# Split weights and stationary tiles that begin at staggered byte offsets in a float32r transformer chain

## The chip, the cores and the metric

The kernel runs on one core of a Trainium2 chip. The metric is the device time of one execution in microseconds (us), median over the runs. TensorE multiplies, ScalarE and VectorE do elementwise work, GpSimd does a few small operations, and SyncE issues most of the transfers. SBUF is the on-chip memory, 128 partitions side by side; an address here is a byte offset within a partition, the same in all of them.

## The reference, cut to what matters

The computation is three transformer layers in a row on 256 tokens of width 1024: a layer with window and neighbourhood attention and an MLP, a layer with retention and an MLP, and a hybrid layer with three attention branches. For the change only their dense products matter, which all have this form:

```python
h = _rmsnorm(x, norm_g)
z = h @ w_in
x = x + y @ w_out
x = x + jnp.square(jax.nn.relu(h @ w1)) @ w2
```

All data are float32. The weights amount to some 42 million numbers and each is used once per execution, for 256 tokens.

## The kernel before, in words

**Split products.** A float32 product is computed as three products in the format float32r, which keeps fewer bits: a number a is split in a_hi (rounded) and a_lo (the rest), and a times b is taken as a_hi b_hi + a_hi b_lo + a_lo b_hi. `mm3` (L329) issues the three matmuls in this order: xh with wh, xh with wl, xl with wh. The activations are the stationary operand (a tile of 128 x 128, loaded by a weight-load instruction ahead of its matmul), and the weights stream past it (128 rows, mostly 512 columns). So in every matmul of a dense layer a slice of `xh` or `xl` (or `hh`, `hl` in the second product of an MLP) is loaded and a slice of a `whi` or `wlo` buffer is streamed.

**Weights.** `plan` (L347) lists the weights in order of use in pieces of 4 x 512 columns (a few of 4 x 256 and 4 x 328). `w_dma` (L392) loads a piece to one of four `raw` buffers over SyncE's queue. A piece is split in two halves, each with two k-tiles. `w_hi` (L424) rounds a half with ScalarE to one of five `whi` buffers, `w_lo` (L438) subtracts with VectorE to one of five `wlo` buffers. `w_get` (L459) hands the slices to the products: the first k-tile of a half begins at column 0 of the buffer, the second at column w (512, 256 or 328). `w_done` (L470) frees a half when the last of the 256 tokens has used it.

**Products.** `panel` (L477) computes 512 output columns (256 or 328 in places) for both token tiles t = 0, 1: k-tiles in groups of two, two and four, for t = 0 and then t = 1. `proj` (L509) and `mlp_out` (L1082) do the products whose k-tiles come in groups of four, with four accumulators. `h_task` (L1051) makes the inner activations of an MLP: ReLU, square, transpose by TensorE (`transpose`, L334, four of 128 x 128 in a row), and split to `hh` and `hl`. `xT_tiles` (L592) makes `xh` and `xl` for a layer's input.

**Order.** A planner written in the kernel (`drive`, L152) runs tasks as generators against a clock of its own and emits instructions in the order in which its cost formulas say that they can start. Costs come from the numbers of columns (`mm`, L324: columns / 2400 + 0.0035 us). Each engine executes its list in order.

**Addresses.** Tiles whose size is a multiple of 2048 bytes per partition lie in a pool of their own (`mt`, L304), a padding tile of 128 bytes stands ahead (L94), and the pools of the layers keep tiles with a multiple of 512 bytes apart from the rest (`Pools`, L43). In the kernel before every `whi`, `wlo`, `raw`, `xh`, `xl`, `hh` and `hl` buffer begins on a multiple of 2048 bytes, and the large tiles of the layers on multiples of 1024. Slices begin at k x 1024 + t x 512 bytes in the stationary tiles and at 0 or 4 w bytes in a weight buffer.

## Time and profile before

| what | value |
|---|---|
| median of the two runs shown | 1022.04 us (1021.53 to 1022.56) |
| the profiled execution's own time | 1021.4 us |
| span of the profiled execution | 1019.6 us |
| mean granted clock of TensorE | 0.997 |
| TensorE, matmuls | 1007.4 us busy, 4962 instructions |
| VectorE | 689.5 us busy, 1133 instructions |
| ScalarE | 536.2 us busy, 817 instructions |
| read from the main memory | 171.69 MB |

The span reaches from the first to the last instruction of the profiled execution; the rest of its time lies around it. PE is TensorE's matmul side, PEld its weight loads, which overlap matmuls, DVE is VectorE, ACT is ScalarE. The records of successive matmuls overlap as well, so the cost of one in a row is read from the distance of two starts and not from its duration. L325 is the line that issues every product, L335 every transpose.

### The profile page before, as it was taken

To read this page: it belongs to the slowest core of one execution; us is meant where nothing else is said; L and a number is where in the kernel's file an instruction comes from. 1 tells how busy PE (TensorE), PEld (TensorE's weight loads), DVE (VectorE), ACT (ScalarE), POOL (GpSimd) and SP (SyncE) were. 2 spreads that over 40 slices of the span, in tenths; PEclk is the share of its full clock that TensorE was granted. 3 is DMA by queue.
4 is the path that set the end of the run, shared out by engine and by line. 5 is a ranking of instruction groups with operands and counts; after the bars stand their busy time and mean duration, and the time that the engine had idled before them with its cause. 6 is when DMAs were issued, how large, how long until landed. Compare 5 with 4: busy or idle time off the path is not lost.

```text
span 1019.6 us, 12930 instructions
## 1 busy us (share of the span) xinstructions
PE 1007.4 (99%) x4962; PEld 835.4 (82%) x4962; DVE 689.5 (68%) x1133; ACT 536.2 (53%) x817; POOL 39.5 (4%) x44
## 2 busy tenths in 40 slices
PE   9989999999999999999999999999999999999997
PEld 7878888888888888888888888888878888888885
DVE  6997666555556977777666555556769857576774
ACT  7766646454445655656445444444555544454453
POOL 1340000000000000000000000000100000000000
PEclk9999999999999999999999999999999999999999
DMA  9733254555554544443545454553624435553531
GB/s 342 224 136 127 89 185 181 188 184 190 188 200 141 206 165 154 173 170 131 200 165 206 166 196 176 197 185 125 205 106 160 171 135 180 201 176 118 203 124 42
DMA packets 27104, 173.58 MB, mean 170 GB/s; under 512 B 3169, under 2 KB 3425, under 8 KB 7585
## 3 DMA queue, kind: packets, MB, share of 16 engines
q1 hardware_dynamic: 25344, 168.05, 46.3%
q0 software_dynamic: 1120, 4.06, 1.7%
q8 instruction: 39, 0.64, 0.2%
q10 hardware_dynamic: 576, 0.64, 0.2%
q14 instruction: 25, 0.20, 0.1%
HBM read 171.69 MB, written 1.05 MB: 169 GB/s over the span
## 4 chain that ended last, share of the span: by engine, by line
PE 95%; DVE 2%; DMA 1%; ACT 1%; issue 0%; POOLq 0%; ACTq 0%; DVEq 0%
PE bank L325 90%; PE bank L335 6%; DMA x<-in_x 1%; DVE p L272 1%; DVE tab L258 0%; DMA cols<-in_cols 0%; ACT p L245 0%; DVE pl L250 0%; DVE p L258 0%; DVE wlo L250 0%; DVE den L250 0%; DVE st L282 0%; DVE qn L250 0%; ACT whi L245 0%; ACT nraw L245 0%
## 5 line engine op out<-in xcount | busy, mean ns | idle before, releaser
L250 DVE TENSOR_TENSOR wlo<-raw,whi 128x1024 fp32r<-128x1024 f32 (+1 forms) x324 | 385.2, 1191 | 184.2 <-ACT whi L245 180.5
L245 ACT ACTIVATE whi<-raw 128x1024 fp32r<-128x1024 f32 (+1 forms) x324 | 333.4, 1033 | 228.4 <-PE bank L325 222.4
L325 PE MATMUL bank<-whi,xh 128*128 128x512 f32 (+2 forms) x848 | 334.0, 396 | 0.1
L325 PE MATMUL bank<-whi,xl 128*128 128x512 f32 (+2 forms) x848 | 326.7, 385 | 0.0
L325 PE MATMUL bank<-wlo,xh 128*128 128x512 f32 (+2 forms) x848 | 326.4, 385 | 0.0
L325 PEld LDWEIGHTS bank<-whi,xh 128*128 128x128 f32 x848 | 159.7, 188 | 31.8 <-issue 3.0
L325 PEld LDWEIGHTS bank<-whi,xl 128*128 128x128 f32 x848 | 159.4, 188 | 32.1
L325 PEld LDWEIGHTS bank<-wlo,xh 128*128 128x128 f32 x848 | 159.9, 189 | 28.0
L325 PE MATMUL bank<-whi,hh 128*128 128x512 f32 x256 | 101.6, 397 | 0.0
L325 PE MATMUL bank<-whi,hl 128*128 128x512 f32 x256 | 100.0, 391 | 0.0
L325 PE MATMUL bank<-wlo,hh 128*128 128x512 f32 x256 | 99.7, 390 | 0.0
L325 PEld LDWEIGHTS bank<-whi,hl 128*128 128x128 f32 x256 | 48.0, 188 | 10.5
L325 PEld LDWEIGHTS bank<-wlo,hh 128*128 128x128 f32 x256 | 48.1, 188 | 9.8
L325 PEld LDWEIGHTS bank<-whi,hh 128*128 128x128 f32 x256 | 48.1, 188 | 9.6
L245 ACT ACTIVATE p<-p,nm 128x256 f32<-128x256 f32 (+1 forms) x64 | 30.2, 473 | 27.1 <-DVE nm L272 26.9
L250 DVE TENSOR_TENSOR hl<-bank,hh 128x512 fp32r<-128x512 f32 x32 | 22.0, 689 | 26.8 <-ACT hh L245 26.8
L245 ACT ACTIVATE hh<-bank 128x512 fp32r<-128x512 f32 x32 | 19.1, 597 | 37.9 <-PE bank L335 37.1
L245 ACT ACTIVATE h<-bank 128x512 f32<-128x512 f32 x32 | 19.2, 599 | 25.4 <-PE bank L325 23.9
L250 DVE TENSOR_TENSOR h<-h,bank 128x512 f32<-128x512 f32 x32 | 21.9, 683 | 14.6 <-ACT h L245 14.4
L325 PE MATMUL bank<-whi,uh 128*128 128x512 f32 x64 | 25.2, 394 | 0.0
L325 PE MATMUL bank<-whi,ul 128*128 128x512 f32 x64 | 25.0, 390 | 0.0
L325 PE MATMUL bank<-wlo,uh 128*128 128x512 f32 x64 | 24.9, 389 | 0.0
(241 smaller groups left out, 1103.7 us busy)
## 6 DMA issues: line engine op xcount, KB each, us to landing
raw<-in_w_mlp_in SPq DMA_DIRECT2D x32, 1024.0 KB, 4.7
raw<-in_w_mlp_out SPq DMA_DIRECT2D x32, 1024.0 KB, 4.7
raw<-in_w_in SPq DMA_DIRECT2D x32, 1024.0 KB, 4.8
raw<-in_w_in_o SPq DMA_DIRECT2D x24, 1024.0 KB, 4.7
raw<-in_w_out_o SPq DMA_DIRECT2D x8, 1024.0 KB, 4.7
raw<-in_w_in_e SPq DMA_DIRECT2D x6, 1024.0 KB, 5.6
raw<-in_w_up SPq DMA_DIRECT2D x6, 1024.0 KB, 4.8
raw<-in_w_mem SPq DMA_DIRECT2D x4, 1024.0 KB, 4.8
```

What stands on the lines that cost most here:

```text
L245: self.nc.scalar.activation(out, in_, func, scale=scale, **kw)
L250: self.nc.vector.tensor_tensor(out, a, b, op=op)
L272: self.nc.vector.tensor_tensor_reduce(out, a, b, scale, init, op0, op1, acc)
L325: self.nc.tensor.matmul(out, lhsT, rhs, start=start, stop=stop)
L335: self.nc.tensor.transpose(out, in_, self.ident)
```

## The change

`moved` allocates a tile with 32 more columns (128 bytes) and returns a view of it that begins `at` columns (4 bytes each) into it. `whi`, `wlo`, `xh`, `xl`, `hh` and `hl` are made with it. Since 128 bytes are added to each buffer, every buffer still begins on a multiple of 128 bytes, and the offset decides where the data begin past it: 0, 16, 32, 64 and 96 bytes for the five hi buffers, 0, 64, 48, 8 and 80 for the five lo buffers, 0 for `xh`, 64 for `xl`, 32 and 96 for the two `hh`, 16 and 64 for the two `hl`.

```diff
+SLACK = 32
+HI_AT, LO_AT = (0, 4, 8, 16, 24), (0, 16, 12, 2, 20)
+HH_AT, HL_AT = (8, 24), (4, 16)
+
+
+def moved(pool, n, dt, name, bufs, at):
+
+    return pool.tile([P, n + SLACK], dt, name=name, tag=name, bufs=bufs)[:, at:at + n]
...
-            hi = self.wp.tile([P, 1024], F32R, name="whi", tag="whi", bufs=self.WB)
+            hi = moved(self.wp, 1024, F32R, "whi", self.WB, HI_AT[n % self.WB])
...
-            lo = self.wp.tile([P, 1024], F32R, name="wlo", tag="wlo", bufs=self.WB)
+            lo = moved(self.wp, 1024, F32R, "wlo", self.WB, LO_AT[n % self.WB])
...
-        return [self.mt([P, 8, S], n, F32R) for n in ("xh", "xl")]
+        return [moved(self.mainp, 2048, F32R, n, 1, at).rearrange("p (k q) -> p k q", k=8)
+                for n, at in (("xh", 0), ("xl", 16))]
...
-                    hTs[j] = [pool.tile([P, 4, S], F32R, name=n, tag=n, bufs=2) for n in ("hh", "hl")]
+                    hTs[j] = [moved(pool, 1024, F32R, n, 2, at[j % 2]).rearrange("p (k q) -> p k q", k=4)
+                              for n, at in (("hh", HH_AT), ("hl", HL_AT))]
```

## Rows read from the trace of the kernel before

**Rows 1.** The page: busy time by engine, and the chain that ended last.
```profile
PE 1007.4 (99%) x4962; PEld 835.4 (82%) x4962; DVE 689.5 (68%) x1133; ACT 536.2 (53%) x817; POOL 39.5 (4%) x44
...
PE 95%; DVE 2%; DMA 1%; ACT 1%; issue 0%; POOLq 0%; ACTq 0%; DVEq 0%
PE bank L325 90%; PE bank L335 6%; DMA x<-in_x 1%; DVE p L272 1%; DVE tab L258 0%; DMA cols<-in_cols 0%; ACT p L245 0%; DVE pl L250 0%; DVE p L258 0%; DVE wlo L250 0%; DVE den L250 0%; DVE st L282 0%; DVE qn L250 0%; ACT whi L245 0%; ACT nraw L245 0%
```

**Rows 2.** Busy time by stretch, instructions of tile whi, then wlo: engine, busy, (count).
```profile
0.00:1020.00 1020.00, 815.68 (x2560) 479.00 (x2560) 385.18 (x324) 333.44 (x324) 1.00 0.48 170
...
0.00:1020.00 1020.00, 494.68 (x1280) 241.14 (x1280) 385.18 (x324) 1.00 0.48 170
```

**Rows 3.** Timeline (start, us), then busy by stretch (PE, PEld, DVE, ACT, POOL; PEclk).
```profile
199.80 0.39 PE L325 MATMUL bank<-whi,hh 128*128 128x512 f32 x1
...
215.22 0.39 PE L325 MATMUL bank<-whi,xl 128*128 128x512 f32 x1
...
199.80:215.22 15.42, 15.42 (x70) 12.76 (x69) 7.97 (x7) 6.17 (x7) 0.00 (x0) 1.00 0.60 204
```

**Rows 4.** Timeline, TensorE, 256-wide panels: one triple, and a settled stretch.
```profile
735.45 0.28 PE L325 MATMUL bank<-whi,xh 128*128 128x256 f32 x1
...
735.79 0.28 PE L325 MATMUL bank<-whi,xh 128*128 128x256 f32 x1
...
740.19 0.28 PE L325 MATMUL bank<-whi,xh 128*128 128x256 f32 x1
...
742.23 0.28 PE L325 MATMUL bank<-whi,xl 128*128 128x256 f32 x1
```

**Rows 5.** Timeline, TensorE, behind four transposes in the first MLP.
```profile
215.45 0.60 PE L335 MATMUL bank<-const,h 128*128 128x128 f32 x4
...
216.12 0.40 PE L325 MATMUL bank<-wlo,xh 128*128 128x512 f32 x1
...
218.43 0.39 PE L325 MATMUL bank<-whi,hl 128*128 128x512 f32 x1
```

**Rows 6.** Timeline, TensorE, first matmul of each triple in the 328-wide panel.
```profile
728.14 0.31 PE L325 MATMUL bank<-whi,xh 128*128 128x328 f32 x1
...
728.59 0.31 PE L325 MATMUL bank<-whi,xh 128*128 128x328 f32 x1
...
729.04 0.31 PE L325 MATMUL bank<-whi,xh 128*128 128x328 f32 x1
...
729.48 0.31 PE L325 MATMUL bank<-whi,xh 128*128 128x328 f32 x1
...
729.93 0.31 PE L325 MATMUL bank<-whi,xh 128*128 128x328 f32 x1
...
730.38 0.31 PE L325 MATMUL bank<-whi,xh 128*128 128x328 f32 x1
...
730.84 0.31 PE L325 MATMUL bank<-whi,xh 128*128 128x328 f32 x1
...
731.28 0.31 PE L325 MATMUL bank<-whi,xh 128*128 128x328 f32 x1
```

**Rows 7.** Groups by form (busy, mean ns | idle), timeline of VectorE, one stretch.
```profile
L250 DVE TENSOR_TENSOR wlo<-raw,whi 128x1024 fp32r<-128x1024 f32 x304 | 371.0, 1223 | 180.0 <-ACT whi L245 176.4
L250 DVE TENSOR_TENSOR wlo<-raw,whi 128x512 fp32r<-128x512 f32 x16 | 10.8, 689 | 3.1 <-ACT whi L245 3.1
L245 ACT ACTIVATE whi<-raw 128x1024 fp32r<-128x1024 f32 x304 | 320.6, 1058 | 216.9 <-PE bank L325 215.0 <-ACT whi L245 0.2
...
724.10 0.84 DVE L250 TENSOR_TENSOR wlo<-raw,whi 128x656 fp32r<-128x656 f32 x1
725.46 0.84 DVE L250 TENSOR_TENSOR wlo<-raw,whi 128x656 fp32r<-128x656 f32 x1 [0.46 <-ACT whi L245]
...
50.00:100.00 50.00, 46.69 (x247) 38.10 (x246) 43.88 (x105) 32.07 (x72) 14.17 (x9) 0.97 0.38 137
```

**Rows 8.** Waits: who waited for whom, us in total, times, longest us.
```profile
ACT whi L245 <- PE bank L325: 222.4, 182, 3.0
```

## The prediction

> **What bounds the kernel now.** The page comes first: TensorE is busy 99% of the span and the chain that ended last is 95% TensorE, 90% of the span by the one line that issues every product; the granted clock of a long stretch reads 1.00, the 2.4 GHz level [rows 1, 3]. So whatever a matmul costs from start to start is the time, and what VectorE and ScalarE do is beside it. The count of matmuls that read the split weights comes next: 2560 with a hi part and 1280 with a lo part streaming, 3840 in all [rows 2]. "Busy" says nothing of what one costs, because the records of successive matmuls overlap: 0.39 us long, they begin 0.23 us apart. The timeline gives the spacing: from 199.80 to 215.22 us, where 70 matmuls overlap the stretch, the first beginning before it and the last at its end, there are 68 spacings in 15.42 us, 226.8 ns each [rows 3]. In the panel that is 256 columns wide 17 spacings take 2.04 us, 120.0 ns each [rows 4]. The difference, 106.8 ns for 256 columns, is 0.417 ns a column, one column per cycle at 2.4 GHz. What is left does not depend on the width: 226.8 - 512 x 0.4167 = 13.4 ns, and 120.0 - 106.7 = 13.3 ns. Each matmul thus pays a fixed 13.3 ns beside its streaming. Over 3840 of them that is 51 us, 5% of the span, and it is all that a shift of addresses can act on, since the columns must be streamed in any case.

> **Is the fixed part rigid?** Behind each group of four transposes the same tiles, at the same addresses, are read at another rhythm: from 216.12 to 218.43 us ten spacings take 2.31 us, 231 ns each, or 17.7 ns over the streaming; after that the spacing is 226.8 ns again until the next transposes [rows 5]. Neither the work nor the addresses differ, only when the streams begin relative to each other. So the fixed part holds a wait on timing between reads, and reads of one memory that are spaced by addresses can be shifted by addresses. Low values occur too: the first 256-wide triple behind the 328-wide panel takes 0.34 us, 113.3 ns a matmul, 6.7 ns over streaming [rows 4].

> **One place of the kernel before already has an offset.** In the 328-wide panel the second k of a half begins 328 x 4 = 1312 bytes into the buffer, 32 bytes past a 128-byte boundary, the first at 0; the stationary tiles stay on the boundary. The panel's triples (xh with hi, xh with lo, xl with hi) alternate between the two. From row to row the three triples at 0 take 0.45, 0.45 and 0.46 us, the four at 32 bytes 0.45, 0.44, 0.45 and 0.44 us, the first of them beginning at 728.14 [rows 6]: 151.1 against 148.3 ns a matmul, 14.4 against 11.7 ns over the 136.7 ns of streaming. That is a difference of 2.8 ns in favour of the offset, from seven triples read to 0.01 us.

> **The change part by part.** It adds and removes no instruction, no DMA and no wait. The planner's costs take column counts, so the order on every engine stays.

> Hi and lo buffers (five each, at 0, 16, 32, 64, 96 and 0, 64, 48, 8, 80 bytes) and xl at 64 and hh, hl at 32, 96 and 16, 64: the streaming starts and the loads of the stationary tile move against each other in all 3840 matmuls, in many combinations. Below, the saving is bounded by the whole 13.3 ns, -51 us; above, by the disturbed spacing as a permanent state, 231 - 226.8 = +4.2 ns, +16 us. The nearest row is the one panel that has an offset, 2.8 ns less. I take it for all: 3840 x 2.8 = 10.8 us. Against the settled 13.3 ns the saving would be 1.6 ns, 6 us; I take the larger because here two sides are staggered, where the panel staggers one.

> Writing and reading these buffers on ScalarE and VectorE: a hi split is 1058 ns, a lo split 1223 ns [rows 7]. In the 328-wide panel the raw half is read at 0 and at 64 bytes past the boundary by turns, and successive lo splits take 0.84 us each [rows 7]: no price. No row has a destination off the boundary, so the bounds are nothing and, from the nearest other pace of the same operation (1223 against 2 x 689 ns for two halves of 512, the overhead paid twice), +0.15 us each. It is hidden in an MLP, where VectorE is busy 7.97 of 15.42 us [rows 3]. The tightest stretch is 50 to 100 us, busy 43.9 [rows 7]: with 324 lo splits in 1020 us [rows 2], some 16 in 50 us, it would gain 2.4 us and reach 46.3, still under 50, and those 2.4 us are the price if that cover is gone. The splits run ahead of TensorE: ScalarE waits 222 us in total for TensorE to free a hi buffer [rows 8], so a slower split first eats that slack. I take 0.

> Memory: 16 buffers x 128 bytes, 2 KB a partition, and everything placed behind moves by multiples of 128 bytes. A 256-byte step already occurs in the heads' value slices inside the same unbroken TensorE chain; I take 0, with the same bounds as the offsets, since no row isolates it.

> Sum: the profiled execution took 1021.4 us for a span of 1019.6; 1021.4 - 10.8 = 1010.6. The median of the runs shown is 1022.0, 0.6 above the profiled one, so 1011.2, rounded to 1011.

> Of the floor under a matmul the trace shows 6.7 ns at best. [...]

> **Rivals.** *Nothing happens.* The fixed 13.3 ns could be the array's own change of weights: it is the same for 256 and 512 columns, and in long stretches it does not move by a nanosecond although the streams of VectorE, ScalarE and the DMAs come and go. Against it stand the disturbed 231 ns. Time: 1022, from 1018 to 1025. [...]

> *The settled rhythm is lost.* Now every stream begins on the same boundary, and the spacing finds 226.8 ns by itself and stays there. With offsets that change from buffer to buffer each matmul could begin in another phase and pay what those behind the transposes pay: 3840 x 4.2 = 16 us, so 1038. It decides for slower as soon as the mean over the pairs exceeds 13.3 ns. For it: the disturbed stretch is the only one at 512 columns whose spacing is not the settled one, and it is dearer. Against it: the 328-wide panel, whose spacings do not settle either, is not dearer.

> *Most of the wait goes.* If the pairs come as low as the 113.3 ns triple, 6.6 ns are saved each, 25 us: 996; at the extreme all 13.3, 971. For it: that triple. Against it: it is one triple, and in the same panels the spacing settles at 120.0 [rows 4].

> **How the numbers follow.** Forecast (1.6 to 5 ns saved, 1003 to 1016) 0.40; most of the wait goes 0.22; nothing 0.20; rhythm lost 0.18. A measurement of this kernel tells about 2%, 20.4 us, from no change: under 1001.6 or over 1042.5. Faster takes the 0.22 of the third rival and 0.02 of the forecast's edge: 0.24. Slower takes a third of the lost rhythm, where the mean passes 5.3 ns: 0.06. Within 2%: 0.70. The range leaves out the extreme of one rival and the dear end of the other: 984 to 1037.

> **What would show it.** If right, a stretch of an MLP without transposes shows spacings of about 224 ns, not one value but a pattern that repeats with the buffers, and the 68 spacings of the stretch in [rows 3] take about 15.2 us; VectorE and ScalarE keep 1223 and 1058 ns. Spacings of 226.8 ns throughout mean that addresses do not matter; 230 and more mean the lost rhythm; below 220, that nearly all the fixed part was a clash of reads. The prediction fails altogether if TensorE begins to wait for splits, which would show as idle time before its matmuls in the groups.

## The result, and the profile after

The changed kernel takes 1035.88 us (1035.38 to 1036.38, two runs) against 1022.04: a ratio of 1.0135 with a 95% interval of 1.0092 to 1.0179. It is slower by 1.35%, where 1011 was forecast. The profiled execution took 1035.38 us for a span of 1033.6, 14.0 us more span than before.

The page of the changed kernel: span, busy time by engine, and the chain that ended last.

```profile
span 1033.6 us, 12930 instructions
...
PE 1021.2 (99%) x4962; PEld 836.6 (81%) x4962; DVE 690.0 (67%) x1133; ACT 536.3 (52%) x817; POOL 39.6 (4%) x44
...
PE 95%; DVE 2%; DMA 1%; ACT 1%; issue 0%; POOLq 0%; ACTq 0%; DVEq 0%
```

Against [rows 1], TensorE has the same 4962 matmuls, the same 99% and the same share of the chain, but 13.8 us more busy time; VectorE and ScalarE differ by 0.5 us at most. There are 12930 instructions as before, and those that do work stand in the same order on every engine. So no new wait and no new work: the same matmuls cost more each.

The groups by form (busy us, mean ns of one, idle time before) for the splits of the changed kernel, which answer to [rows 7]:

```profile
L261 DVE TENSOR_TENSOR wlo<-raw,whi 128x1024 fp32r<-128x1024 f32 x304 | 370.9, 1222 | 186.5 <-ACT whi L256 185.4
L256 ACT ACTIVATE whi<-raw 128x1024 fp32r<-128x1024 f32 x304 | 320.5, 1057 | 224.9 <-PE bank L336 221.4 <-DVE sg L277 1.4 <-ACT whi L256 0.2
```

1222 and 1057 ns, before 1223 and 1058: writing at 8 to 96 bytes past a multiple of 128 costs the splits nothing. ScalarE still waits for TensorE to free a hi buffer, and the view of waits (us in total, times, longest us) has 229.1 us in place of the 222.4 of [rows 8]:

```profile
ACT whi L256 <- PE bank L336: 229.1, 179, 3.1
```

Now the cost of one matmul. The chain in order of time (start us, us, what) has twelve pieces of 78 consecutive products in the MLPs. One such piece of the kernel before:

```profile
197.89 17.72 PE bank L325 x78
```

and the same piece of the changed kernel:

```profile
200.23 18.07 PE bank L336 x78
```

All twelve took 17.72 us before, 227.2 ns for each of the 78; now they take 18.04 to 18.10, 231.7 ns each in the one shown. The timeline of TensorE in that piece of the changed kernel, start us and length us, the first three and the last two of 15 matmuls in a row:

```profile
204.70 0.39 PE L336 MATMUL bank<-whi,hl 128*128 128x512 f32 x1
204.93 0.40 PE L336 MATMUL bank<-whi,hh 128*128 128x512 f32 x1
205.16 0.39 PE L336 MATMUL bank<-wlo,hh 128*128 128x512 f32 x1
...
207.71 0.40 PE L336 MATMUL bank<-whi,xh 128*128 128x512 f32 x1
207.94 0.39 PE L336 MATMUL bank<-wlo,xh 128*128 128x512 f32 x1
```

3.24 us for 14 spacings are 231.4 ns each, where the stretch of [rows 3] had 226.8. This is the rhythm that stood behind the transposes in [rows 5], and here it does not go over into 226.8. Taken over all start times of the trace, the 3557 spacings between one 512-column matmul and the next average 231.2 ns before and 234.9 ns after. 3.7 ns times 3557 is 13.2 us, nearly all of the 14.0 by which the span grew. Of the spacings far (over 12 matmuls) behind anything else, 2284 of the 3557, the mean is 226.7 before and 231.5 after.

So the place of the loss is plain. Which part of the change makes it is not: the edit does two things to the addresses. It adds offsets under 128 bytes, and by adding 128 bytes to 16 buffers it moves the buffers behind them. By the places that the program gives its tiles, the buffers' bases modulo 256 become 0, 0, 128, 0, 128 for the five hi buffers, 128, 128, 0, 128, 0 for the five lo buffers, 128 for `xl`, 0 and 128 for the two `hh` and the two `hl`, while `xh` stays at 0. Before, all were 0. With the offsets on top, 3408 of the 3696 matmuls of 512 columns have a streamed and a stationary operand that differ modulo 256; before, none had.

### The profile page after: what moved, and what is told of

It is laid out like the page before. It is cut to its first block, busy times and chain, and to the rows that moved or that the text cites. A ratio compares the mean times of both kernels' runs of the same rounds, so it can differ in the third digit from the quotient of the medians.

```text
span 1033.6 us, 12930 instructions
## 1 busy us (share of the span) xinstructions
PE 1021.2 (99%) x4962; PEld 836.6 (81%) x4962; DVE 690.0 (67%) x1133; ACT 536.3 (52%) x817; POOL 39.6 (4%) x44
## 4 chain that ended last, share of the span: by engine, by line
PE 95%; DVE 2%; DMA 1%; ACT 1%; issue 0%; POOLq 0%; ACTq 0%; DVEq 0%
PE bank L336 90%; PE bank L346 6%; DMA x<-in_x 1%; DVE p L283 1%; DVE tab L269 0%; DMA cols<-in_cols 0%; ACT p L256 0%; DVE pl L261 0%; DVE p L269 0%; DVE den L261 0%; DVE wlo L261 0%; DVE st L293 0%; DVE qn L261 0%; ACT whi L256 0%; ACT nraw L256 0%
## 5 line engine op out<-in xcount | busy, mean ns | idle before, releaser
L256 ACT ACTIVATE whi<-raw 128x1024 fp32r<-128x1024 f32 (+1 forms) x324 | 333.3, 1032 | 236.9 <-PE bank L336 229.1
```

The costliest lines, as they stand in the source:

```text
L256: self.nc.scalar.activation(out, in_, func, scale=scale, **kw)
```

## The experiments

The kernel before was run beside each group; its median there was 1022.13 us (7 runs) and 1022.18 (16 runs), and ratios are to those.

**1. Keep the 128 bytes, take all offsets away.**

```diff
-HI_AT, LO_AT = (0, 4, 8, 16, 24), (0, 16, 12, 2, 20)
-HH_AT, HL_AT = (8, 24), (4, 16)
+HI_AT, LO_AT = (0, 0, 0, 0, 0), (0, 0, 0, 0, 0)
+HH_AT, HL_AT = (0, 0), (0, 0)
...
-                for n, at in (("xh", 0), ("xl", 16))]
+                for n, at in (("xh", 0), ("xl", 0))]
```

> The 128 bytes are added to every buffer, but all offsets are 0, so every buffer begins on a multiple of 128 bytes and no longer of 2048. Theory A (the offset past a 128-byte boundary breaks the settled rhythm of 226.7 ns per 512-column matmul): the time of the kernel before, 1022 us, within 3 us, spacings of 226.7 ns. Rival B (it is the loss of the 512- and 2048-byte alignment): 1036 us, spacings near 231.5 ns.

Measured: 1033.87 us, ratio 1.0113 (1.0098 to 1.0128). The same piece of its chain:

```profile
199.03 18.04 PE bank L336 x78
```

With every tile on a multiple of 128 bytes, 11.7 us of the loss are still there, and the spacing far behind anything else is 231.5 ns as in the full change. The theory that the offsets under 128 bytes are needed for the loss falls. The part that the prediction had costed at nothing is enough by itself.

**2 and 3. The offsets of one side only.** Both keep the added 128 bytes. The first has offsets on the streamed weights alone, the second on the stationary tiles alone.

```diff
-HH_AT, HL_AT = (8, 24), (4, 16)
+HH_AT, HL_AT = (0, 0), (0, 0)
...
-                for n, at in (("xh", 0), ("xl", 16))]
+                for n, at in (("xh", 0), ("xl", 0))]
```

> The weight buffers keep the offsets of the change, the stationary tiles begin at 0 past the boundary. Theory A with the streaming side as the cause: 1033 to 1037 us, most of the loss. Rival C (it is the stationary side's weight load that falls out of step): near 1022 us.

```diff
-HI_AT, LO_AT = (0, 4, 8, 16, 24), (0, 16, 12, 2, 20)
+HI_AT, LO_AT = (0, 0, 0, 0, 0), (0, 0, 0, 0, 0)
```

> The stationary tiles keep their offsets (0 and 64, 32 and 96, 16 and 64 bytes), the weight buffers begin at 0. If the streaming side is the cause: 1022 to 1025 us. Rival C (stationary side): near 1036 us. If both sides count and only their difference matters: about 1027, since xh and xl stay at multiples of 64.

Measured: 1035.83 us, ratio 1.0130 (1.0113 to 1.0147), and 1036.76, 1.0142 (1.0126 to 1.0157). The two do not tell the sides apart, since experiment 1 has shown that what they share, the 128 bytes, already costs 11.7 us. What they show is that offsets on either side on top of it add little (2.0 and 2.9 us over experiment 1), and that the costs do not add up. The expectations' numbers say little here, since they reckon without the moved bases.

**4. The spacing by itself, first attempt.** Behind the kernel's own work, sections of 48 matmuls follow, with tiles of their own. A section has one setting of offsets.

```diff
...
+            for sa, sb, n, seq in BENCH:
+                for i in range(48):
+                    m = mv[seq[i % len(seq)]]
+                    self.mm(ps[:, :n], st["ab"[i % 2], (sa, sb)[i % 2]], m[:, :n], True, True)
...
```

> The kernel before with sections of 48 matmuls of 512 columns at its end, in which nothing else runs: all moving operands at one offset (0, 16, 32, 64, 8 bytes), two by turns (0 with 8, 16, 32, 48, 64, 80, 96, 112), the stationary tile at 16, 32, 64, or by turns, triples, and narrower matmuls of 508 to 480 columns. The output is the reference's; the added part is some 300 us. Theory A: one offset for all gives 226.7 ns whatever it is; by turns it does not settle and costs 229 to 236 ns, except 0 with 64 or 0 with 0. Rival D (VectorE, ScalarE or transfers that meet the weight buffers at other addresses make the difference): 226.7 ns in all sections of 512 columns.

Measured: no section of 512 columns settled at 226.7 ns. All lie between 229.3 and 234.2, the one without any offset too (232.2). The fault is in the experiment: its tiles have sizes that are no multiple of 256 bytes and so uneven bases, one stationary tile at 128 and the other at 0 modulo 256, so that "no offset" was not "alike". That gives it a use after all. The kernel gives VectorE and ScalarE nothing to do beside these sections, so the dear spacing is not a clash with other engines; the rows of experiment 5 show both at 0.00 us busy beside spacings of 233 ns.

**5. The same with known addresses.** Two streamed and two stationary tiles, each on a multiple of 2048 bytes, used from a slice that begins at a chosen number of bytes.

```diff
...
+            for n, m, s, count in BENCH:
+                for i in range(count):
+                    a, b = m[i % len(m)] // 4, s[i % len(s)] // 4
+                    self.mm(ps[:, :n], st[i % 2][:, b:b + P], mv[i // 3 % 2][:, a:a + n], True, True)
...
```

> The kernel before with sections of 48 matmuls at its end in which nothing else runs, this time with all four tiles on 2048-byte boundaries and the operands moved by slices: moving operand at 0, 128, 256, 512, 1024, 64, 32, 16 or 8 bytes with the stationary at 0, the stationary at 128, 256, 512, 64, 32, 16 with the moving at 0, both moved alike, two values by turns, and 256 columns. The output is the reference's. Theory E (the settled rhythm of 226.7 ns needs both operands on a boundary larger than 128 bytes, and which one the base decides): 226.7 ns in the sections where all offsets are 0, 512 or 1024, and 229 to 234 ns in those at 128 and at less. Theory A (only what lies under 128 bytes counts, or only that all start alike): 226.7 ns at 128 and 256 as well. Rival F (the rhythm depends on the instructions around and not on addresses at all): no section differs from the first by more than 1 ns.

Mean spacing over the last 24 of each section, 512 columns, M the streamed and S the stationary tile's bytes past the boundary:

| section | ns | section | ns |
|---|---|---|---|
| M 0, S 0 | 226.7 | M 0, S 128 | 233.3 |
| M 128, S 0 | 233.3 | M 0, S 256 or 512 | 226.7 |
| M 256, 512 or 1024, S 0 | 226.7 | M 0, S 64, 32 or 16 | 233.3 |
| M 64, S 0 | 228.9 | both at 128, 256, 64 or 32 | 226.7 |
| M 32 or 8, S 0 | 233.3 | both at 16 | 231.1 |
| M 16, S 0 | 231.7 | M by turns 0 and 128 | 230.0 |
| M by turns 0 and 256 or 512 | 226.7 | M by turns 0 and 64, 32 or 16 | 230.8, 230.0, 231.7 |
| S by turns 0 and 256 or 512 | 226.7 | S by turns 0 and 128 or 64 | 232.2, 230.0 |

Busy time by stretch, one section a row, in the order M0 S0, M128 S0, M256 S0, then S128, then both at 128 (the stretch, its length, PE, PEld, DVE, ACT and POOL busy, granted clock, DMA share, GB/s):

```profile
1038.60:1049.48 10.88, 10.88 (x49) 9.01 (x48) 0.00 (x0) 0.00 (x0) 0.00 (x0) 1.00 0.00 0
1049.48:1060.67 11.19, 11.19 (x49) 9.01 (x48) 0.00 (x0) 0.00 (x0) 0.00 (x0) 1.00 0.00 0
1060.67:1071.57 10.90, 10.90 (x50) 9.01 (x48) 0.00 (x0) 0.00 (x0) 0.00 (x0) 1.00 0.01 2
...
1137.85:1149.03 11.18, 11.18 (x49) 9.01 (x48) 0.00 (x0) 0.00 (x0) 0.00 (x0) 1.00 0.00 0
...
1204.41:1215.33 10.92, 10.92 (x49) 9.01 (x48) 0.00 (x0) 0.00 (x0) 0.00 (x0) 1.00 0.01 2
```

A section has 48 spacings: 10.88 us are 226.7 ns each, 11.19 are 233.1 (a count of 49 or 50 takes in records that overlap the ends). VectorE, ScalarE and GpSimd are idle, the clock reads 1.00 and the loads are busy for the same 9.01 us in all. The rows say that it is not a boundary that counts: a shift of 128 costs 6.7 ns if one operand has it and nothing if both have it, and a shift of 256 or 512 costs nothing on either side, nor 1024 on the streamed one. What counts is whether the streamed and the stationary operand begin at the same address modulo 256 bytes. None of the expectations holds as it was written: theory E wanted a boundary larger than 128 bytes, theory A had a shift of 128 harmless, rival F had no section differ. From here on theory E means likeness modulo 256. The loads overlap the products in the dear sections as in the others (9.01 us of loads beside 11.19 and 10.88 us of products), and the place of one operand relative to the other is worth 6.7 ns a matmul all the same; by what means, no run shows.

**6. The changed kernel with its operands brought back to the same address modulo 256.** The 128 bytes stay, and every tile whose base is at 128 modulo 256 gets an offset of 128 bytes (32 columns).

```diff
-HI_AT, LO_AT = (0, 4, 8, 16, 24), (0, 16, 12, 2, 20)
-HH_AT, HL_AT = (8, 24), (4, 16)
+HI_AT, LO_AT = (0, 0, 32, 0, 32), (32, 32, 0, 32, 0)
+HH_AT, HL_AT = (0, 32), (0, 32)
...
-                for n, at in (("xh", 0), ("xl", 16))]
+                for n, at in (("xh", 0), ("xl", 32))]
```

> The change with other numbers: every offset is 0 or 128 bytes, chosen so that base plus offset is a multiple of 256 for each weight buffer and each stationary tile. Theory E (the rhythm settles at 226.7 ns when moving and stationary operand lie alike modulo 256 bytes, whatever the offsets are called): all of the loss is undone, 1022 us within 3 us, although buffers have the added 128 bytes and lie no longer on 512 or 2048. Rival B (the loss of the 512- and 2048-byte boundaries): 1033 us or more. Rival G (the added 2 KB and the places of the other tiles): 1033 us.

Measured: 1022.04 us, ratio 0.9998 (0.9989 to 1.0007). Its chain:

```profile
197.86 17.72 PE bank L336 x78
```

17.72 us, as before, in all twelve pieces. The whole loss is undone, with the same 2 KB added and with the weights no longer on multiples of 512 or 2048. So it is neither the larger buffers nor the lost larger boundaries.

**7. The weights at 128, the stationary tiles at 0 modulo 256,** and **8. both at 128.**

```diff
-HI_AT, LO_AT = (0, 4, 8, 16, 24), (0, 16, 12, 2, 20)
-HH_AT, HL_AT = (8, 24), (4, 16)
+HI_AT, LO_AT = (32, 32, 0, 32, 0), (0, 0, 32, 0, 32)
+HH_AT, HL_AT = (0, 32), (0, 32)
...
-                for n, at in (("xh", 0), ("xl", 16))]
+                for n, at in (("xh", 0), ("xl", 32))]
```

> The same with the opposite numbers for the weight buffers: all of them at 128 modulo 256, the stationary tiles at 0 modulo 256. Theory E: every weight matmul at 233.3 ns; 3696 x 6.7 = 24.6 us at most, less where the rhythm was disturbed anyway, so 1040 to 1047 us, slower than the change itself. Theory A and rival B: no slower than the slack alone, 1034 us.

```diff
-HI_AT, LO_AT = (0, 4, 8, 16, 24), (0, 16, 12, 2, 20)
-HH_AT, HL_AT = (8, 24), (4, 16)
+HI_AT, LO_AT = (32, 32, 0, 32, 0), (0, 0, 32, 0, 32)
+HH_AT, HL_AT = (32, 0), (32, 0)
...
-                for n, at in (("xh", 0), ("xl", 16))]
+                for n, at in (("xh", 32), ("xl", 0))]
```

> As the run with the weights at 128 modulo 256, but with xh, xl, hh and hl at 128 as well. The other stationary tiles (of the retention output, the attention outputs, the memory projection and the branches' up projection) stay at 0, so 552 of 3840 matmuls remain unlike. Theory E (the difference counts, not the place): 1022 to 1028 us. If the place of the moving operand counts by itself: 1040 us or more.

Measured: 1038.27 us, ratio 1.0155 (1.0141 to 1.0169), for the first, and 1025.71, 1.0032 (1.0020 to 1.0044), for the second. The piece of the chain in the first:

```profile
200.03 18.13 PE bank L336 x78
```

and in the second:

```profile
199.66 17.74 PE bank L336 x78
```

With one side at 128 a piece costs 232.4 ns a matmul, with both sides there 227.4. It is the difference that counts. The first came out a little under its range: far behind anything else its spacing is 232.4 in the kernel where the section had 233.3. In the second, 528 of the 3696 matmuls of 512 columns have stationary tiles that the edit does not move (`uh` and others; with 24 of the 328-wide panel, unlike in the kernel before too, that makes the 552 of the expectation). They stay unlike, at 232.4 ns, and 528 x 5.7 = 3.0 us are most of the 3.5 that it is slower.

**9. The kernel before with offsets on the hi buffers alone.** All bases stay on multiples of 256.

```diff
-            hi = self.wp.tile([P, 1024], F32R, name="whi", tag="whi", bufs=self.WB)
+            at = (0, 4, 8, 16, 24)[n % self.WB]
+            hi = self.wp.tile([P, 1024 + 64], F32R, name="whi", tag="whi", bufs=self.WB)[:, at:at + 1024]
```

> The kernel before with 256 bytes added to the five hi buffers and the change's hi offsets (0, 16, 32, 64, 96 bytes); lo buffers and stationary tiles as before on multiples of 256. Here the offsets under 128 bytes stand alone, without a shift of 128 by the added space. Theory E: some 2050 of 3840 matmuls are unlike and the others around them do not settle, 1029 to 1035 us. Rival H (offsets under 128 bytes do nothing, the shift by the added 128 bytes did it all): 1022 us.

Measured: 1036.02 us, ratio 1.0133 (1.0119 to 1.0147), 1 us above the range. Three of its four runs had a mean granted clock of 0.994; the fourth, at 0.997, took 1034.97. Its chain:

```profile
201.24 18.08 PE bank L325 x78
```

Four of five hi buffers at 16 to 96 bytes are as dear as the whole change. So offsets under 128 bytes do the harm too, without any help from the moved bases; the change does it twice over, and the second time costs little (1033.9 with the one, 1036.0 with the other, 1035.9 with both).

Why half a change costs as much as a whole one can be read from the trace and the places of the tiles. In this run 1968 of the 3696 matmuls of 512 columns are unlike, and the alike ones between them are hardly cheaper: far behind anything else the mean distance to the next start is 231.8 ns for an unlike matmul and 231.2 for an alike one. An alike matmul with an unlike one ahead of it has 232.3; the fourth to sixth in a row 227.3 to 228.7, and from the seventh on 226.5 to 227.2. So the loss is not a price on each unlike matmul: it is the rhythm of the whole stream, which comes back only after several alike ones, as it does behind the transposes of [rows 5]. In experiment 1, where 1912 are unlike and hardly ever more than three alike stand in a row, it never comes back: 231.4 ns for the alike ones.

**10. Which pair must be alike.** Sections as in 5. By turns of 0 and 128, either each matmul's own two operands are unlike and the next load is like the running stream, or the reverse. Further sections look for a setting below 226.7 ns and at other widths.

```diff
+BENCH = [(512, (0,), (0,), 64)] + [(512, m, s, 48) for m, s in (
+    ((0,), (0,)), ((0, 128), (128, 0)), ((0, 128), (0, 128)), ((0, 64), (64, 0)), ((0, 64), (0, 64)),
...
+    (n, m, s, 48) for n in (448, 384, 320, 256) for m, s in (((0,), (0,)), ((128,), (0,)))]
...
```

> Sections of 48 matmuls with nothing beside them, as in the run on boundaries. First, which stationary tile counts while an operand streams: moving at 0 and 128 by turns with the stationary at 128 and 0 (own pair unlike, the pair of the stream and the next load alike) and at 0 and 128 (own pair alike, next unlike). Theory E1 (the load that runs beside the stream, that of the next matmul): 226.7 ns in the first, about 230 or more in the second. Theory E2 (the matmul's own pair): the other way round. Then the moving operand at 48 to 240 bytes in steps that were not tried, stationary at 0: by theory E all at 229 to 234 ns; one below 226.7 would be a better setting than any of the kernels has. Then both alike at 48, 80, 96, 8 and 160, and 288 with 32 bytes: 226.7 ns, 8 bytes perhaps not, as 16 with 16 did not settle. Last, 448, 384, 320 and 256 columns alike and at 128: alike columns x 0.4167 + 13.3 ns, that is 200.0, 173.3, 146.7 and 120.0 ns; at 128 more for 448 and 384, about the same or less at 256, where 118.6 ns was seen.

Busy time by stretch, TensorE alone, one section a row: all alike; own pair unlike; own pair alike and next load unlike; both at 80; both at 96.

```profile
1039.03:1049.92 10.89, 10.89 (x50) 1.00 0.00 0
1049.92:1060.97 11.05, 11.05 (x50) 1.00 0.00 0
1060.97:1071.93 10.96, 10.96 (x49) 1.00 0.01 1
...
1205.78:1216.83 11.05, 11.05 (x50) 1.00 0.01 1
1216.83:1227.75 10.92, 10.92 (x49) 1.00 0.00 0
```

Neither expectation held alone: 230.0 ns with the own pair unlike and 228.3 with the next load unlike (233.3 and 231.7 with 64 in place of 128). So neither likeness gives 226.7 without the other. Which of the two pairs makes the loss, these rows do not tell, since the addresses also change from matmul to matmul here, and by experiment 9 even a matmul that is alike in both ways is dear among unlike ones. Of the offsets tried, alike is enough only on multiples of 32 bytes: both at 96, both at 160, or the streamed one at 288 and the stationary one at 32 give 226.7, both at 80, 48, 16 or 8 give 230.0 to 231.1. Nine more offsets of the streamed tile against a stationary one at 0 (48 to 240 bytes) give 230.0 to 234.3; no setting at 512 columns came below 226.7, so these runs point to no version that beats the kernel before. The widths:

| columns | alike, ns | streamed at 128, ns |
|---|---|---|
| 448 | 202.8 | 203.7 |
| 384 | 173.3 | 176.1 |
| 320 | 146.7 | 146.7 |
| 256 | 120.0 | 118.6 |

## Why the prediction was wrong

**What bounds the kernel:** right. The spacing of the matmuls is the time, and 3.7 ns on 3557 of the spacings, 13.2 us, is nearly all of the loss. The streaming share is measured as well: 106.8 ns between 256 and 512 columns are 0.417 ns a column, 2.4 columns a nanosecond, at a granted clock of 1.00 [rows 3, 4], and the alike sections of experiment 10 have 106.7 ns. The 2.4 GHz of the forecast stands for this rate; the profile has the clock as a share of full speed alone.

**The splits and the order cost nothing:** right. 1222 and 1057 ns, the same order, and TensorE busy for 99% of the span as before. One reading was off without effect: the tightest of the stretches of 50 us in the kernel before is 750 to 800 us, where VectorE is busy 44.84 us, not 50 to 100 with its 43.88.

**"The fixed part holds a wait on timing between reads":** right as far as it goes. Addresses alone, with the same instructions, move the spacing from 226.7 to 233.3 ns. Behind the transposes the disturbed rhythm of 231 ns wears off at the same addresses (226.7 ns far behind anything else); with unlike addresses it does not (231.5 ns). That one read waits for another stays an inference. Left out was what [rows 3 to 5] could also have said: 226.8 is the low end of the two rhythms seen at 512 columns, and a kernel whose matmuls of 512 columns all have operands that begin alike already has it wherever its stream is long.

**The step that failed: "The nearest row is the one panel that has an offset, 2.8 ns less. I take it for all".** The sign was wrong: in place of 2.8 ns saved on each of 3840 matmuls, the change adds 3.7 ns on average and 4.8 where the stream is long. The panel of [rows 6] has 328 columns. In experiment 10 the price of an offset (of 128 bytes there) hangs on the width: at 256 columns the unlike pair is 1.4 ns cheaper, at 320 there is no difference, at 384, 448 and 512 it is 2.8, 0.9 and 6.7 ns dearer. A row of 328 columns stands where the sign turns, and says nothing of 512, which nearly all matmuls have. Nor did the panel show a saving at its own width. The three triples at 0 that the four at 32 bytes were held against run in the same disturbed stream. From the trace's starts in ns the seven triples take 3.147 us, 149.9 ns a matmul or 13.2 over the streaming, about the settled 13.3 again: what the triples at 32 bytes gain, those at 0 lose. (The difference itself is 1.8 ns in these starts, 149.1 against 150.9; the 2.8 came of rounding to 0.01 us.) The rows that did have 512 columns in an unsettled state, [rows 5], were used as an upper bound only.

**The second step that failed: "everything placed behind moves by multiples of 128 bytes ... I take 0".** Experiment 1 measures it at +11.7 us; the term was given the offsets' bounds, but went into the sum as nothing. The 256-byte step that the text gave for cover is, by experiment 5, exactly the step that costs nothing; half of it costs 6.7 ns a matmul.

**The rivals.** *The settled rhythm is lost* is what happened: its 231 ns for each matmul against a measured 231.5, its 1038 us against 1035.9, and its sign (230 and more) in the profile. It is 2 us high, since the 1273 spacings near transposes and other work were dear already (239.3 ns before, 241.1 after), and since its 3840 matmuls include 144 narrower ones. It had 0.18, since the 328-wide panel was held against it. That 1035.9 lies within 984 to 1037 is no merit of the forecast: the range reached so far up for this rival alone. *Nothing happens* falls by the interval of the ratio, *most of the wait goes* by the sign; the 113.3 ns triple has nothing like it among the sections of 256 columns (118.6 to 120.0).

**What stays open.** The runs show which addresses settle, not what in the chip makes the period of 256 bytes and the grain of 32. They do not explain why the spacing is dearer by steps (228.9 with the streamed tile at 64, 233.3 with the stationary one there), nor the fixed 13.3 ns that is left when all is alike. The change's own offsets on bases that are all multiples of 256 were not tried for all buffers; experiment 9 does it for the hi buffers. Why the alike pair needs a stretch of alike ones around it is open too.

## What to carry to other kernels

Where float32r products of 512 columns follow each other without a gap, let the stationary and the streamed tiles begin at the same address modulo 256 bytes, on multiples of 32 (226.7 ns each, against 228.3 to 234.3 otherwise); here that was worth 1.1 to 1.6% of the time. In experiment 9 four unlike buffers of ten were enough to lose it all. Padding one tile moves all that are placed behind it, so look at base plus offset and not at the offset. Read the price from the distance of two starts in a long undisturbed stretch, and carry a price over only to matmuls of the same width: an offset of 128 bytes cost 6.7 ns at 512 columns and saved 1.4 ns at 256.
